# Softmax cross entropy over 32000 classes: labels' load behind the table load, last sums in PSUM, last pieces in multiples of 256 bytes, eight semaphores fewer

## Chip, cores, metric

One core of one Trainium2 chip. The metric is the device time of one execution in microseconds, lower is better. All runs were fast, granted clock 1.0.

## The reference

```python
batch, seq, vocab = 16, 512, 32000          # logits float32, labels int32
logits_max = np.max(logits, axis=-1, keepdims=True)
log_sum_exp = np.log(np.sum(np.exp(logits - logits_max), axis=-1)) + logits_max.squeeze(-1)
log_probs = logits - log_sum_exp[..., np.newaxis]
loss = -log_probs[np.arange(batch)[:, None], np.arange(seq), labels]
```

8192 rows of 32000 logits are read once, 1048.6 MB. The kernel leaves out the maximum (the logits are normal draws) and computes log(sum(exp(x))) - x[label].

## The kernel before

Each of the 128 partitions has 64 rows, "groups" here. A group is loaded in two loads of 16000 columns, into three buffers of 64 kB per partition in turn. ScalarE takes the exp in place and adds it up into one column of `sums`, for which an accumulator read (ACTIVATION_READ_ACCUMULATOR in the profiles) follows each exp; GpSimd picks the labels' logits out of the buffer before that. The first group comes in four loads. The last two groups are cut into ever smaller pieces, so that little is left to do when the last byte has landed.

```python
    plan(0, [[4000, 4000, 8000], [16000]], [(0, 0), (0, 1), (0, 2), (1, 0)])
    for g in range(1, G - 2):
        plan(g, [[W], [W]], [(0, 0), (1, 0)])
    b = loads[-1][1] + 1
    for g, i, at, n in [                    # group, buffer, first column in it, columns
        (G - 2, 0, 0, 12000), (G - 2, 1, 0, 11000), (G - 2, 2, 0, 9000),
        (G - 1, 3, 0, 8720), (G - 1, 2, 9000, 6470), (G - 1, 3, 8720, 4700),
        (G - 1, 4, 0, 3410), (G - 1, 3, 13420, 2550), (G - 1, 4, 3410, 1910), (G - 1, 4, 5320, 1455),
        (G - 1, 4, 6775, 1135), (G - 1, 4, 7910, 905), (G - 1, 4, 8815, 745),
    ]:
        loads.append((g, b + i, at, n))
    # ... cut ...
    sums = persist.tile([P, G - 1, 5], FP32)
    sums_last = persist.tile([P, K], FP32)              # K = 10 pieces of the last group
    # ... cut ...
    nc.scalar.dma_start(out=labs64[:], in_=labels_pg)
    nc.scalar.preload_act_table_set("natural_log_exp_and_others")
    # ... cut: indices, lists and masks for picking the labels' logits ...
    def exp(g, ap):
        k = n_exp.get(g, 0)
        n_exp[g] = k + 1
        s = sums[:, g, k:k + 1] if g < G - 1 else sums_last[:, k:k + 1]
        return nc.scalar.activation(out=ap, in_=ap, func=EXP, accum_out=s)

    for j, (g, b, at, n) in enumerate(loads):
        # ... cut ...
        load = nc.sync.dma_start(out=t[:, at:at + n], in_=lg_pg[:, g, c0:c0 + n])
        if n == W:                                      # three semaphores for full loads,
            n_full[b % 3] += 1                          # one more for each short load
            loaded = (full_in[b % 3], 16 * n_full[b % 3])
        else:
            loaded = (tc.alloc_semaphore(f"short{j}_in"), 16)
        # ... cut: pick on GpSimd, exp on ScalarE, waits ...
        left = len(loads) - 1 - j
        if left == 9:
            nc.vector.reduce_sum(out=totals[:], in_=sums[:], axis=X)
            # ... cut ...
        if left == 8:
            nc.scalar.activation(out=logsum[:], in_=totals[:], func=LN)
            # ... cut ...
        if left == 1:
            nc.vector.reduce_sum(out=part[:], in_=sums_last[:, 0:K - 1], axis=X)
    nc.sync.dma_start(out=out_pg[:, 0:G - 1], in_=res[:])

    nc.scalar.activation(out=logsum_last[:], in_=sums_last[:, K - 1:K], func=LN, bias=part[:])
    nc.vector.tensor_tensor(out=res_last[:], in0=logsum_last[:], in1=lab_logit[:, G - 1:G], op=ALU.subtract)
    nc.sync.dma_start(out=out_pg[:, G - 1:G], in_=res_last[:])
```

The softmax here doesn't subtract the row's maximum and nothing guards it: scores larger than these inputs give would overflow.

Of the kernel before, what the change touches and what calls it, by code (L numbers as in the profile page):

```python
# [9 lines left out]
FP32 = mybir.dt.float32  # L10
# [4 lines left out]
LN = mybir.ActivationFunctionType.Ln  # L15
ALU = mybir.AluOpType
X = mybir.AxisListType.X
# [3 lines left out]
def kernel(  # L21
# [6 lines left out]
    nc = tc.nc  # L28

    B, S, V = logits.shape  # L30
    P = 128
    G = B * S // P
    W = 16000
# [9 lines left out]
    loads = []  # L43

    def plan(g, widths_by_buffer, order):

        n_buffers = 1 + max((l[1] for l in loads), default=-1)
        for b, i in order:
            ws = widths_by_buffer[b]
            loads.append((g, n_buffers + b, sum(ws[:i]), ws[i]))  # L50

    plan(0, [[4000, 4000, 8000], [16000]], [(0, 0), (0, 1), (0, 2), (1, 0)])
    for g in range(1, G - 2):
        plan(g, [[W], [W]], [(0, 0), (1, 0)])
    b = loads[-1][1] + 1
    for g, i, at, n in [
        (G - 2, 0, 0, 12000), (G - 2, 1, 0, 11000), (G - 2, 2, 0, 9000),
        (G - 1, 3, 0, 8720), (G - 1, 2, 9000, 6470), (G - 1, 3, 8720, 4700),
        (G - 1, 4, 0, 3410), (G - 1, 3, 13420, 2550), (G - 1, 4, 3410, 1910), (G - 1, 4, 5320, 1455),
        (G - 1, 4, 6775, 1135), (G - 1, 4, 7910, 905), (G - 1, 4, 8815, 745),  # L60
    ]:
        loads.append((g, b + i, at, n))
    assert sum(l[3] for l in loads) == G * V


    ends = ctx.enter_context(tc.tile_pool(name="ends", bufs=1))
# [2 lines left out]
    persist = ctx.enter_context(tc.tile_pool(name="persist", bufs=1))  # L69
# [26 lines left out]
    in_first = persist.tile([P, G], mybir.dt.int32)  # L96
    picks = ctx.enter_context(tc.tile_pool(name="picks", bufs=2))
    K = 10
    sums = persist.tile([P, G - 1, 5], FP32)
    sums_last = persist.tile([P, K], FP32)  # L100
    totals = persist.tile([P, G - 1], FP32)
    logsum = persist.tile([P, G - 1], FP32)
    res = persist.tile([P, G - 1], FP32)
    part = persist.tile([P, 1], FP32)
    logsum_last = persist.tile([P, 1], FP32)
    res_last = persist.tile([P, 1], FP32)

    ctx.enter_context(tc.manual_schedule())


    nc.scalar.dma_start(out=labs64[:], in_=labels_pg)
    nc.scalar.preload_act_table_set("natural_log_exp_and_others")  # L112
    nc.vector.memset(sums[:], 0.0)  # L113
    nc.gpsimd.iota(idx[:], pattern=[[V, G]], base=0, channel_multiplier=G * V)
    nc.gpsimd.tensor_tensor(out=idx[:], in0=idx[:], in1=labs32, op=ALU.add)  # L115
    nc.gpsimd.iota(part16[:], pattern=[[0, 1]], base=0, channel_multiplier=1)
    nc.gpsimd.iota(entries[:], pattern=[[1, NI]], base=0, channel_multiplier=0, allow_small_or_imprecise_dtypes=True)
    for g in gathered:
        nc.gpsimd.indirect_dma_start(  # L119
            out=lab_logit[:, g:g + 1],  # L120
            out_offset=None,
            in_=lg,
# [6 lines left out]
    for q in range(3):  # L129
        nc.vector.tensor_scalar(  # L130
            out=mine[:, q:q + 1], in0=part16f[:], scalar1=4.0 * q, scalar2=None, op0=ALU.add
        )
    for n in (12.0, 6.0):
        nc.vector.tensor_scalar(  # L134
            out=mine_at[:], in0=mine[:], scalar1=n, scalar2=n, op0=ALU.is_ge, op1=ALU.mult
# [3 lines left out]
    for q in range(3):  # L139
        nc.vector.tensor_scalar(  # L140
            out=mine_at[:, q:q + 1], in0=mine[:, q:q + 1], scalar1=16.0 * q, scalar2=None, op0=ALU.mult
# [4 lines left out]
        out=one_hot[:], in0=entries[:], scalar1=at_entry[:], scalar2=None, op0=ALU.is_equal  # L146
    )
    nc.vector.tensor_scalar(
        out=clamped[:, 0, :], in0=labs32, scalar1=float(W - 1), scalar2=None, op0=ALU.min
    )  # L150
    nc.vector.tensor_scalar(
        out=clamped[:, 1, :], in0=labs32, scalar1=float(-W), scalar2=0.0, op0=ALU.add, op1=ALU.max
    )
    nc.vector.tensor_scalar(
        out=in_first[:], in0=labs32, scalar1=float(W), scalar2=None, op0=ALU.is_lt
    )
    for h in range(2):
        for q in range(3):
            nc.vector.tensor_scalar(  # L159
                out=lists[:, :, h, q], in0=clamped[:, h, :], scalar1=mine[:, q:q + 1], scalar2=None, op0=ALU.mult  # L160
# [6 lines left out]
    buffers = {}  # L167
    col = {}
    n_exp = {}
    full_in = [tc.alloc_semaphore(f"full{i}_in") for i in range(3)]  # L170
    n_full = [0, 0, 0]
    spaces = [data.tile([P, W], FP32, tag=f"t{i}", name=f"t{i}") for i in range(3)]
    exps = []

    def exp(g, ap):
        k = n_exp.get(g, 0)
        n_exp[g] = k + 1
        s = sums[:, g, k:k + 1] if g < G - 1 else sums_last[:, k:k + 1]
        return nc.scalar.activation(out=ap, in_=ap, func=EXP, accum_out=s)  # L179

    for j, (g, b, at, n) in enumerate(loads):
        if b not in buffers:
            buffers[b] = spaces[b % 3]
        t = buffers[b]
        c0 = col.get(g, 0)
        col[g] = c0 + n
        load = nc.sync.dma_start(out=t[:, at:at + n], in_=lg_pg[:, g, c0:c0 + n])  # L187
        if n == W:
            n_full[b % 3] += 1
            loaded = (full_in[b % 3], 16 * n_full[b % 3])  # L190
        else:
            loaded = (tc.alloc_semaphore(f"short{j}_in"), 16)
        load.then_inc(loaded[0], 16)
        tc.no_tile_sem_insts.add(load.ins.name)
        users = []
        if g in picked:
            h = c0 // W
            i = picked.index(g) % NB
            if h == 0 and i == 0:
                pk = picks.tile([P, NB * 2, NI], FP32, tag="pk", name="pk")  # L200
            pick = nc.gpsimd.indirect_copy(  # L201
                out=pk[:, 2 * i + h, :], data=t[:], idxs=lists[:, g, h, 0:3], i_know_this_is_slow=True
            )
            users.append(pick)
        users.append(exp(g, t[:, at:at + n]))
        users[0]._wait_ge(*loaded)
        tc.add_to_no_dep_group(f"load{j}", load.ins)
        tc.declare_no_dep(users[0].ins, load.ins, reason="waits for the load's own semaphore")
        tc.declare_fence(users[0].ins, group=f"load{j}")
        exps.append(users[-1])  # L210
        if g in picked and h == 1 and i == NB - 1:
            nc.vector.copy_predicated(own[:], one_hot[:].unsqueeze(1).to_broadcast([P, NB * 2, NI]), pk[:])  # L212
            nc.vector.reduce_sum(  # L213
                out=found[:, :, g - NB + 1:g + 1].rearrange("p h g -> p g h"),
                in_=own[:].rearrange("p (g h) n -> p g h n", h=2),
                axis=X,
# [5 lines that stand above are left out]
            lo, hi = picked[0], picked[-1] + 1  # L222
            nc.vector.tensor_copy(out=lab_logit[:, lo:hi], in_=found[:, 1, lo:hi])
            nc.vector.copy_predicated(lab_logit[:, lo:hi], in_first[:, lo:hi], found[:, 0, lo:hi])  # L224
        if left == 8:
            nc.scalar.activation(out=logsum[:], in_=totals[:], func=LN)  # L226
            nc.vector.tensor_tensor(out=res[:], in0=logsum[:], in1=lab_logit[:, 0:G - 1], op=ALU.subtract)  # L227
        if left == 1:
            nc.vector.reduce_sum(out=part[:], in_=sums_last[:, 0:K - 1], axis=X)  # L229
    assert n_exp[G - 1] == K  # L230
    nc.sync.dma_start(out=out_pg[:, 0:G - 1], in_=res[:])

    nc.scalar.activation(out=logsum_last[:], in_=sums_last[:, K - 1:K], func=LN, bias=part[:])  # L233
    nc.vector.tensor_tensor(out=res_last[:], in0=logsum_last[:], in1=lab_logit[:, G - 1:G], op=ALU.subtract)  # L234
    nc.sync.dma_start(out=out_pg[:, G - 1:G], in_=res_last[:])

# [29 lines left out]
```

## Time and profile before

| | kernel before |
|---|---|
| time, median of the first 3 runs | 2426.2 us (2426.05 to 2426.23) |
| span of the profiled execution | 2424.19 us |
| that execution's time less its span | 2.20 us |
| mean distance of the landings of full loads (8.19 MB) | 18.87 us |
| last full load landed, last load landed | 2344.10, 2420.18 us |

The span goes from the program's first recorded instruction to its last; the time of a run also holds what the runtime does around it. Landings are the moments at which a load's semaphore, the counter that its transfer raises, is full; they come from the trace's semaphore records, and an exp that waited for data starts 0.02 us after one.

From the page of the kernel before: the span, the chain that ended last by engine, and the issue-to-landing time of the full loads.

```profile
span 2424.2 us, 667 instructions
...
DMA 71%; ACT 23%; issue 4%; POOL 1%; SPq 0%; POOLq 0%; DVE 0%
...
t<-in_logits_dram SPq DMA_DIRECT2D x123, 8000.0 KB, 41.5
```

The chain's 71% for DMA is a lower bound: while it walks over an exp, the transfers go on. 41.5 us from issue to landing is 2.2 times the 18.87 us that a load takes, so two others stand ahead of it in the queue, one of them nearly done.

The start, in order of time (start, duration, engine and line, operation, output and input; in brackets the idle time before it and what ended it):

```profile
0.73 0.40 ACTq L111 DMA_DIRECT2D labs<-in_labels_dram  x1
...
1.16 1.28 ACT L112 ACT_TABLE_LOAD   x1 [1.16 <-PEq L250]
...
8.51 0.32 POOL L115 TENSOR_TENSOR idx<-idx,labs 128x64 int32<-128x64 int32 x1 [7.48 <-DMA labs<-in_labels_dram]
```

The labels' load is issued first, the table load after it, and the labels are there at 8.5 us. The last full load's exp, from the same view, later:

```profile
2344.13 13.54 ACT L179 ACTIVATE t<-t 128x16000 f32<-128x16000 f32 x1 [5.26 <-DMA t<-in_logits_dram]
```

It started as its load landed.

### The profile page before, as it was taken

The page shows a single profiled execution, that of the slowest core. Times are in us where ns is not written, and L with a number is a line of the kernel's source. Part 1 is how long each engine was busy: PE and PEld are TensorE (multiplying, and loading weights), DVE is VectorE, ACT ScalarE, POOL GpSimd, SP SyncE. Part 2 cuts the span into 40 slices and gives each one's busy share as a digit, 9 for nine tenths or more (in the row PEclk, how much of TensorE's full clock was granted, in tenths as well). Part 3 has the DMA queues.
Part 4 walks back from the last instruction along what each step waited for, and adds up shares of the span by engine and source line. Part 5 has one row for each costly group of instructions (what it writes and reads, how often), then busy time and mean ns, then how long its engine had stood idle before and what let it go on. Part 6 is the DMA issues. An engine that isn't in the chain of part 4 may idle for free.

```text
span 2424.2 us, 667 instructions
## 1 busy us (share of the span) xinstructions
DVE 20.5 (1%) x45; ACT 1748.6 (72%) x281; POOL 86.6 (4%) x132
## 2 busy tenths in 40 slices
DVE  0000000000000000000000000000000000000000
ACT  4777767777677767777677776777767776777778
POOL 0000000000000000000000000000000000000000
DMA  9999999999999999999999999999999999999999
GB/s 424 438 423 439 439 423 438 439 430 432 439 437 425 439 438 423 439 438 429 434 439 436 426 439 436 426 439 437 429 435 438 434 429 438 437 426 439 437 430 384
DMA packets 20580, 1048.72 MB, mean 433 GB/s; under 512 B 2656, under 2 KB 2784, under 8 KB 3424
## 3 DMA queue, kind: packets, MB, share of 16 engines
q1 hardware_dynamic: 20304, 1048.62, 99.9%
q10 hardware_dynamic: 144, 0.07, 0.0%
q0 software_dynamic: 128, 0.00, 0.0%
q14 instruction: 4, 0.03, 0.0%
HBM read 1048.64 MB, written 0.03 MB: 433 GB/s over the span
## 4 chain that ended last, share of the span: by engine, by line
DMA 71%; ACT 23%; issue 4%; POOL 1%; SPq 0%; POOLq 0%; DVE 0%
DMA t<-in_logits_dram 71%; ACT t L179 23%; POOL pk L201 1%; SPq L187 0%; POOLq L261 0%; ACT logsum_last L233 0%; ACT logsum L226 0%; DVE res_last L234 0%; POOLq L201 0%
## 5 line engine op out<-in xcount | busy, mean ns | idle before, releaser
L179 ACT ACTIVATE t<-t 128x16000 f32<-128x16000 f32 (+6 forms) x139 | 1734.7, 12480 | 671.8 <-POOL pk L201 630.9
L201 POOL INDIRECT_COPY pk<-t,lists 128x48 f32 x120 | 81.6, 680 | 2211.8 <-DMA t<-in_logits_dram 2211.8
L212 DVE COPY_PREDICATED own<-one_hot,pk 128x960 f32<-128x960 int32 x6 | 7.4, 1235 | 2281.7 <-POOL pk L201 2281.7
L179 ACT ACTIVATION_READ_ACCUMULATOR t<-t 128x1 f32 x139 | 25.9, 186 | 0.0
L213 DVE TENSOR_REDUCE found<-own 128x20 f32<-128x960 f32 x6 | 6.9, 1155 | 0.2
L119 POOL DMA_INDIRECT lab_logit<-in_logits_dram,idx x4 | 4.1, 1032 | 1.3 <-issue 0.9
L112 ACT ACT_TABLE_LOAD x1 | 1.3, 1283 | 1.2 <-PEq L250 1.2
L159 DVE TENSOR_SCALAR lists<-clamped,mine 128x64 uint16<-128x64 f32 x6 | 1.2, 362 | 0.0
L221 DVE TENSOR_REDUCE totals<-sums 128x63 f32<-128x315 f32 x1 | 0.5, 481 | 79.4 <-ACT t L179 79.4
L162 DVE MEMSET own<- 128x960 f32 x1 | 0.9, 858 | 0.1
L115 POOL TENSOR_TENSOR idx<-idx,labs 128x64 int32<-128x64 int32 x1 | 0.3, 319 | 7.5 <-DMA labs<-in_labels_dram 7.5
L145 DVE TENSOR_SCALAR one_hot<-entries,at_entry 128x48 int32<-128x48 f32 x1 | 0.4, 355 | 0.1
L227 DVE TENSOR_TENSOR res<-logsum,lab_logit 128x63 f32<-128x63 f32 x1 | 0.2, 225 | 15.2 <-ACT logsum L226 15.2
L134 DVE TENSOR_SCALAR mine_at<-mine 128x3 f32<-128x3 f32 x2 | 0.3, 169 | 0.1
L113 DVE MEMSET sums<- 128x315 f32 x1 | 0.3, 321 | 0.9 <-PEq L250 0.9
L137 DVE TENSOR_TENSOR mine<-mine,mine_at 128x3 f32<-128x3 f32 x2 | 0.3, 163 | 0.1
L233 ACT ACTIVATE logsum_last<-sums_last,part 128x1 f32<-128x1 f32 x1 | 0.3, 294 | 0.0
L229 DVE TENSOR_REDUCE part<-sums_last 128x1 f32<-128x9 f32 x1 | 0.2, 163 | 14.5 <-ACT t L179 14.5
L140 DVE TENSOR_SCALAR mine_at<-mine 128x1 f32<-128x1 f32 x3 | 0.3, 148 | 0.0
L130 DVE TENSOR_SCALAR mine<-part16f 128x1 f32<-128x1 f32 x3 | 0.3, 147 | 0.0
L226 ACT ACTIVATE logsum<-totals 128x63 f32<-128x63 f32 x1 | 0.2, 238 | 0.0
L224 DVE COPY_PREDICATED lab_logit<-in_first,found 128x60 f32<-128x60 int32 x1 | 0.2, 231 | 0.0
(17 smaller groups left out, 2.7 us busy)
## 6 DMA issues: line engine op xcount, KB each, us to landing
t<-in_logits_dram SPq DMA_DIRECT2D x123, 8000.0 KB, 41.5
t<-in_logits_dram SPq DMA_DIRECT2D x1, 6000.0 KB, 36.8
t<-in_logits_dram SPq DMA_DIRECT2D x1, 5500.0 KB, 32.3
t<-in_logits_dram SPq DMA_DIRECT2D x1, 4500.0 KB, 24.1
t<-in_logits_dram SPq DMA_DIRECT2D x1, 4360.0 KB, 23.6
t<-in_logits_dram SPq DMA_DIRECT2D x2, 2000.0 KB, 9.6
t<-in_logits_dram SPq DMA_DIRECT2D x1, 4000.0 KB, 21.2
t<-in_logits_dram SPq DMA_DIRECT2D x1, 3235.0 KB, 30.9
```

The source lines that it names most:

```text
L112: nc.scalar.preload_act_table_set("natural_log_exp_and_others")
L113: nc.vector.memset(sums[:], 0.0)
L115: nc.gpsimd.tensor_tensor(out=idx[:], in0=idx[:], in1=labs32, op=ALU.add)
L119: nc.gpsimd.indirect_dma_start(out=lab_logit[:, g:g + 1], out_offset=None, in_=lg, in_offset=bass.IndirectOffsetOnAxis(ap=idx[:, g:g + 1], ...
L145: nc.vector.tensor_scalar(out=one_hot[:], in0=entries[:], scalar1=at_entry[:], scalar2=None, op0=ALU.is_equal)
L159: nc.vector.tensor_scalar(out=lists[:, :, h, q], in0=clamped[:, h, :], scalar1=mine[:, q:q + 1], scalar2=None, op0=ALU.mult)
L162: nc.vector.memset(own[:], 0.0)
L179: return nc.scalar.activation(out=ap, in_=ap, func=EXP, accum_out=s)
L201: pick = nc.gpsimd.indirect_copy(out=pk[:, 2 * i + h, :], data=t[:], idxs=lists[:, g, h, 0:3], i_know_this_is_slow=True)
L212: nc.vector.copy_predicated(own[:], one_hot[:].unsqueeze(1).to_broadcast([P, NB * 2, NI]), pk[:])
L213: nc.vector.reduce_sum(out=found[:, :, g - NB + 1:g + 1].rearrange("p h g -> p g h"), in_=own[:].rearrange("p (g h) n -> p g h n", h=2), a ...
L221: nc.vector.reduce_sum(out=totals[:], in_=sums[:], axis=X)
```

## The change

Its intent: start the logits' load before the labels', save the overhead of two loads, make every piece begin and end on 256 bytes, make ScalarE's accumulator reads at the end cheaper by writing them to PSUM in place of SBUF, the core's other on-chip memory (in banks of their own, so that VectorE can sum one part while ScalarE writes another), fit the pieces to the cheaper reads, and leave the closing clear fewer semaphores.

```diff
-    plan(0, [[4000, 4000, 8000], [16000]], [(0, 0), (0, 1), (0, 2), (1, 0)])
-    for g in range(1, G - 2):
+    for g in range(G - 2):
         plan(g, [[W], [W]], [(0, 0), (1, 0)])
@@
-        (G - 2, 0, 0, 12000), (G - 2, 1, 0, 11000), (G - 2, 2, 0, 9000),
-        (G - 1, 3, 0, 8720), (G - 1, 2, 9000, 6470), (G - 1, 3, 8720, 4700),
-        (G - 1, 4, 0, 3410), (G - 1, 3, 13420, 2550), (G - 1, 4, 3410, 1910), (G - 1, 4, 5320, 1455),
-        (G - 1, 4, 6775, 1135), (G - 1, 4, 7910, 905), (G - 1, 4, 8815, 745),
+        (G - 2, 0, 0, 11264), (G - 2, 1, 0, 10752), (G - 2, 2, 0, 9984),
+        (G - 1, 3, 0, 9152), (G - 1, 3, 9152, 6656), (G - 1, 2, 9984, 4736),
+        (G - 1, 4, 0, 3392), (G - 1, 4, 3392, 2496), (G - 1, 4, 5888, 1728), (G - 1, 4, 7616, 1408),
+        (G - 1, 4, 9024, 1024), (G - 1, 4, 10048, 768), (G - 1, 4, 10816, 640),
@@
-    sums = persist.tile([P, G - 1, 5], FP32)
-    sums_last = persist.tile([P, K], FP32)
+    psum = ctx.enter_context(tc.tile_pool(name="psum", bufs=1, space=bass.MemoryType.PSUM))
+    sums = persist.tile([P, G - 1, 3], FP32)
+    sums_last = psum.tile([P, 8, 512], FP32, tag="sums_last", name="sums_last")
+    place_last = [(max(0, k - 2), min(k, 2) if k <= 2 else 0) for k in range(K)]
@@
+    nc.scalar.preload_act_table_set("natural_log_exp_and_others")
     nc.scalar.dma_start(out=labs64[:], in_=labels_pg)
-    nc.scalar.preload_act_table_set("natural_log_exp_and_others")
     nc.vector.memset(sums[:], 0.0)
+    nc.vector.memset(sums_last[:, :, 0:K - 7], 0.0)
@@
-        s = sums[:, g, k:k + 1] if g < G - 1 else sums_last[:, k:k + 1]
+        if g < G - 1:
+            s = sums[:, g, k:k + 1]
+        else:
+            bank, at = place_last[k]
+            s = sums_last[:, bank, at:at + 1]
@@
-        if n == W:
-            n_full[b % 3] += 1
-            loaded = (full_in[b % 3], 16 * n_full[b % 3])
+        if at == 0:
+            count_in[b % 3] += 16
+            loaded = (first_in[b % 3], count_in[b % 3])
         else:
-            loaded = (tc.alloc_semaphore(f"short{j}_in"), 16)
+            loaded = (tc.alloc_semaphore(f"load{j}_in"), 16)
@@
-            nc.vector.reduce_sum(out=part[:], in_=sums_last[:, 0:K - 1], axis=X)
+            nc.vector.reduce_sum(out=partial[:], in_=sums_last[:, 0:7, 0:K - 7], axis=mybir.AxisListType.XY)
@@
-    nc.scalar.activation(out=logsum_last[:], in_=sums_last[:, K - 1:K], func=LN, bias=part[:])
+    nc.scalar.activation(out=logsum_last[:], in_=sums_last[:, 7, 0:1], func=LN, bias=partial[:])
```

(Names of tiles and an assertion are cut.) The pieces 0, 1 and 2 of the last group share bank 0; pieces 3 to 9 have banks 1 to 7.

More of the change, by code (lines that the diff above doesn't have):

```diff
@@ L56 @@
     for g, i, at, n in [
-        (G - 2, 0, 0, 12000), (G - 2, 1, 0, 11000), (G - 2, 2, 0, 9000),
-        (G - 1, 3, 0, 8720), (G - 1, 2, 9000, 6470), (G - 1, 3, 8720, 4700),
-        (G - 1, 4, 0, 3410), (G - 1, 3, 13420, 2550), (G - 1, 4, 3410, 1910), (G - 1, 4, 5320, 1455),
-        (G - 1, 4, 6775, 1135), (G - 1, 4, 7910, 905), (G - 1, 4, 8815, 745),
+        (G - 2, 0, 0, 11264), (G - 2, 1, 0, 10752), (G - 2, 2, 0, 9984),
+        (G - 1, 3, 0, 9152), (G - 1, 3, 9152, 6656), (G - 1, 2, 9984, 4736),
+        (G - 1, 4, 0, 3392), (G - 1, 4, 3392, 2496), (G - 1, 4, 5888, 1728), (G - 1, 4, 7616, 1408),
+        (G - 1, 4, 9024, 1024), (G - 1, 4, 10048, 768), (G - 1, 4, 10816, 640),
     ]:
         loads.append((g, b + i, at, n))
-    assert sum(l[3] for l in loads) == G * V
+    assert sum(l[3] for l in loads) == G * V and all(l[2] % 64 == l[3] % 64 == 0 for l in loads)
     ends = ctx.enter_context(tc.tile_pool(name="ends", bufs=1))
@@ L103 @@
     res = persist.tile([P, G - 1], FP32)
-    part = persist.tile([P, 1], FP32)
+    partial = persist.tile([P, 1], FP32)
     logsum_last = persist.tile([P, 1], FP32)
@@ L169 @@
     n_exp = {}
-    full_in = [tc.alloc_semaphore(f"full{i}_in") for i in range(3)]
-    n_full = [0, 0, 0]
+    first_in = [tc.alloc_semaphore(f"first{i}_in") for i in range(3)]
+    count_in = [0, 0, 0]
     spaces = [data.tile([P, W], FP32, tag=f"t{i}", name=f"t{i}") for i in range(3)]
-    exps = []
     def exp(g, ap):
@@ L209 @@
         tc.declare_fence(users[0].ins, group=f"load{j}")
-        exps.append(users[-1])
         if g in picked and h == 1 and i == NB - 1:
```

## The prediction

> **What bounds the kernel now.** I read the page first (busy shares, transfer rate), then the waits, then the order of time at both ends, then the packet records under it.
>
> From the page:
>
> ```profile
> DVE 20.5 (1%) x45; ACT 1748.6 (72%) x281; POOL 86.6 (4%) x132
> ...
> DMA  9999999999999999999999999999999999999999
> GB/s 424 438 423 439 439 423 438 439 430 432 439 437 425 439 438 423 439 438 429 434 439 436 426 439 436 426 439 437 429 435 438 434 429 438 437 426 439 437 430 384
> ...
> q1 hardware_dynamic: 20304, 1048.62, 99.9%
> ```
>
> No engine is near full, and the transfers are busy in every slice. The logits are 8192 x 32000 x 4 B = 1048.6 MB, read once; only the last slice, with 384 GB/s, is below the rest. So the time is: first byte, 1048.6 MB at the rate of the transfers, then what is left after the last byte. The queue of the loads, from the waits of SyncE:
>
> ```profile
> SPq L187 <- ACT t L179: 2333.3, 126, 26.4
> ```
>
> The loads are issued when the exp of a buffer ends, but they take 41.5 us to land while 8.2 MB take 18.87 us (mean distance of landings in the trace), so two loads always stand in the queue and this wait costs nothing. The chain of waits gives 71% to the transfers and 23% to the exps because it walks from an exp to the load that it released; it must not be read as 23% of exps to be saved.
>
> The tail, in order of time:
>
> ```profile
> 2392.22 7.47 ACT L179 ACTIVATE t<-t 128x8720 f32<-128x8720 f32 x1 [2.54 <-DMA t<-in_logits_dram]
> 2399.60 0.19 ACT L179 ACTIVATION_READ_ACCUMULATOR t<-t 128x1 f32 x1
> 2399.90 5.59 ACT L179 ACTIVATE t<-t 128x6470 f32<-128x6470 f32 x1
> 2405.40 0.19 ACT L179 ACTIVATION_READ_ACCUMULATOR t<-t 128x1 f32 x1
> 2405.50 0.24 ACT L226 ACTIVATE logsum<-totals 128x63 f32<-128x63 f32 x1
> 2405.64 4.10 ACT L179 ACTIVATE t<-t 128x4700 f32<-128x4700 f32 x1
> ...
> 2420.23 0.18 ACT L179 ACTIVATION_READ_ACCUMULATOR t<-t 128x1 f32 x1
> 2420.32 0.81 ACT L179 ACTIVATE t<-t 128x745 f32<-128x745 f32 x1
> 2420.45 0.16 DVE L229 TENSOR_REDUCE part<-sums_last 128x1 f32<-128x9 f32 x1 [14.46 <-ACT t L179]
> 2421.04 0.18 ACT L179 ACTIVATION_READ_ACCUMULATOR t<-t 128x1 f32 x1
> 2421.26 0.29 ACT L233 ACTIVATE logsum_last<-sums_last,part 128x1 f32<-128x1 f32 x1
> 2421.58 0.16 DVE L234 TENSOR_TENSOR res_last<-logsum_last,lab_logit 128x1 f32<-128x1 f32 x1 [0.97 <-ACT logsum_last L233]
> 2421.77 0.34 SPq L235 DMA_DIRECT2D out_dram<-res_last  x1
> ```
>
> The reader is to see that ScalarE waits for data before the 8720 piece and has no gap from the 6470 piece on. By the landing records the 6470 piece landed at 2399.88 and the 745 piece at 2420.18, so each of the last eight exps starts 0.10 to 0.20 us after its data: the tail is balanced between transfers and ScalarE, with ScalarE 0.14 us late at the end. Everything that is left to save is: under 1 us there, some tenths of transfer time, some tenths at the two ends.
>
> **What the Trainium skill says.** (1) "Perfetto Trace Analysis", Optimizing Scalar/DVE Operations: a ScalarE operation carries about 93 ns of data access on SBUF and about 51 on PSUM, and the latency in a profile is about twice that. The trace agrees for SBUF: an accumulator read is 186 ns long, and the next exp starts 93 ns after it. That PSUM is shorter no run has shown yet. (2) "DMA: Bandwidth & Descriptors", How a descriptor splits into AXI transactions: pieces go in units of 256 B, and a start off such a boundary fetches unused bytes. The packet records agree in kind: 64000 B take 2361 ns and 16000 B 596, so a packet costs 7.7 ns + 0.03677 ns/B; the off-boundary 2980 B should then take 117 and take 122, 3620 B 141 and take 142, 13640 B 509 and take 511. (3) The same page, Queues, rings and completion order: an engine alternates between its queues packet by packet. Below. (4) "PSUM — Partial Sum Buffer", PSUM bank collisions raise a hardware error: two engines must not touch one bank at once. So the VectorE sum of the first pieces and the last accumulator go to different banks; no cost follows.
>
> **The change part by part.** A load is 128 rows on 16 DMA engines, 8 packets each.
>
> - *First group in two loads in place of four.* Before, buffer 0 took per engine 8 x (596 + 596 + 1185) = 19.02 us, now 8 x 2361 = 18.89. On the path: -0.13 us. The first exp moves from 8.2 us to about 21 us (1.75 for the first packet + 0.5 of slow first packets + 18.9); ScalarE has 5.2 us idle per load and its buffer is needed again at about 58 us, so nothing follows.
> - *Labels behind the table load.* They are 512 B packets, nine per engine with the completion, 27 ns each: 0.24 us of transfer time in either place. They now alternate with 2.36 us packets in place of 0.6 us ones, so they should land near 9 x 2.4 + 2.5 = 24 us (8.2 before). First use at 61 us: hidden. The first logits packet came 1.0 us after its issue with the labels issued beside it; the last store, alone, also took 0.95. At most -0.06 us; I take -0.02.
> - *Multiples of 256 B.* Excess over the line 7.7 + 0.03677 B times 8, summed over the last pieces: 38 (745), 8 (905), 3, 3, 10 and less, about 0.1 us in all. The landing of the last piece: -0.1 us.
> - *Accumulators in PSUM.* An exp with its read occupies ScalarE for N/1.2 ns + 186 (4700: 4.10; 1910: 1.78). If PSUM shortens the read's share from 93 to 51, that is N/1.2 + 144. The new sizes say that this was assumed: the old ones follow "exp of a piece = transfer of the next" at 186 ns within 30 columns, the new ones do so at about 130 to 145.
> - *The new sizes.* I ran the tail by hand: a piece starts at its landing + 0.02 or when ScalarE is free; 0.14 for the logarithm of the other groups after the second piece. Old sizes, 186: the last exp with its read is done 0.93 us after the last landing (the trace: 0.95, at 2421.13). New sizes: at 144, 0.95; at 186, 1.33; at 131, 0.83. The first three accumulators share a bank, and the order of instructions shows that the second and third exp now wait for the one before to be complete; the second waits for its data anyway, the third may lose about 0.05. So I expect 0.98: +0.03.
> - *The last logarithm.* The accumulator read before it should be 144 long in place of 186, and the logarithm (294) reads PSUM: -0.08. VectorE's sum over seven banks is longer than 163 ns but has 0.6 us.
> - *Eight semaphores fewer.* The kernel's closing clear of its semaphores takes 222 ns for about 33; 8 of them: -0.05 us if it is proportional.
>
> Sum: -0.13 - 0.02 - 0.10 + 0.03 - 0.08 - 0.05 = -0.35. From 2426.2: **2425.85 us**.
>
> **The rivals.** *PSUM shortens only the write's end, not ScalarE's period.* For it: the accumulator read has no source operand in the trace, and the 93 ns may belong to the reading side. Then the new sizes are wrong for the machine, the tail grows by 0.38 in place of 0.03 and the time is about 2426.2. I give it three in ten. *The tail gets shorter than I think:* period 100 ns or less over N/1.2; by the same hand run the end is then 0.65 after the last landing, and the time 2425.5. Against it: nothing in the skill goes so low. *The labels or the four gathers disturb the large packets*, since they now lie beside 64 kB packets: their bytes are the same, so I give this little; it would cost some tenths. *The new order starves the queue at the end:* the load of 3392 columns waits for the exp of 10752, done near 2379, when more than 25 us of transfers are still queued; so no.
>
> **Range and chances.** The three runs of before lie within 0.2 us. The sum of my uncertain terms is about 0.5 us either way, and another chip may add some: 2425.0 to 2426.7. A change of 2% is 48 us; nothing here reaches it unless the bandwidth changes, so within 2% 0.99, faster 0.005, slower 0.005.
>
> **What would show it.** In the profile of after: 20016 packets on the logits' queue (139 transfers x 144) with the same distance of 18.87 us between landings; labels landing near 24 us; accumulator reads of the last group near 144 ns, with the next exp about 51 ns after the read's start (93 would mean the first rival); the last exp starting 0.2 to 0.35 us after its landing; last logarithm near 250 ns; semaphore clear under 200 ns. I am wrong if the loads' rate differs, if ScalarE's lateness grows from piece to piece past 0.4 us, or if a wait for the piece before costs more than 0.1 us.

## The result

The changed kernel took 2425.90 us (median of 6 runs, 2425.80 to 2425.97); the kernel before 2426.23 in the same rounds (6 runs, 2426.05 to 2426.60). The ratio, computed as the mean time of one kernel's fast runs over that of the other's of the same rounds and so not quite the ratio of these medians, is 0.9998, with an interval of 0.9985 to 1.0011. The measured 2425.90 lies within 0.05 us of the forecast of 2425.85. Whether for the forecast's reasons is the rest of this document.

The page after: the span, the transfer rate in 40 slices, and the logits' queue.

```profile
span 2424.1 us, 663 instructions
...
GB/s 424 437 425 439 439 423 438 439 428 434 439 435 427 439 436 426 439 439 427 435 439 433 429 439 435 427 439 438 425 438 438 431 432 438 435 428 439 436 426 389
...
q1 hardware_dynamic: 20016, 1048.62, 99.9%
```

139 transfers of 144 packets: 20016. But the span has shrunk by only 0.12 us (2424.19 to 2424.07 in the trace's own figures), the time of these two executions by 0.49. 2.20 us of the kernel before lay outside the span, 1.83 of the changed one.

The start, in order of time:

```profile
0.73 1.28 ACT L114 ACT_TABLE_LOAD   x1 [0.73 <-PEq L256]
...
0.77 0.39 ACTq L115 DMA_DIRECT2D labs<-in_labels_dram  x1
...
22.84 0.32 POOL L119 TENSOR_TENSOR idx<-idx,labs 128x64 int32<-128x64 int32 x1 [21.82 <-DMA labs<-in_labels_dram]
```

The sequencer does not wait for the table load: the labels' load is issued 0.04 us later than before. GpSimd has the labels at 22.8 us in place of 8.5, because their small packets now take turns with packets of 64 kB. The Trainium skill's "DMA: Bandwidth & Descriptors", Queues, rings and completion order, says that an engine changes between its queues at packet boundaries, and this is that: from 4.66 us on, the labels' queue gets one packet per engine every 2.38 us, eight times, with the completion in the last turn (the prediction counted nine).

The tail, in order of time:

```profile
2343.91 13.54 ACT L186 ACTIVATE t<-t 128x16000 f32<-128x16000 f32 x1 [5.24 <-DMA t<-in_logits_dram]
...
2400.23 0.15 ACT L186 ACTIVATION_READ_ACCUMULATOR t<-t 128x1 f32 x1
2400.47 5.75 ACT L186 ACTIVATE t<-t 128x6656 f32<-128x6656 f32 x1
2406.13 0.15 ACT L186 ACTIVATION_READ_ACCUMULATOR t<-t 128x1 f32 x1
2406.18 0.24 ACT L232 ACTIVATE logsum<-totals 128x63 f32<-128x63 f32 x1
2406.37 4.15 ACT L186 ACTIVATE t<-t 128x4736 f32<-128x4736 f32 x1
...
2420.30 0.20 ACT L186 ACTIVATION_READ_ACCUMULATOR t<-t 128x1 f32 x1
2420.36 0.78 ACT L186 ACTIVATE t<-t 128x640 f32<-128x640 f32 x1
...
2420.98 0.21 ACT L186 ACTIVATION_READ_ACCUMULATOR t<-t 128x1 f32 x1
2421.22 0.26 ACT L239 ACTIVATE logsum_last<-sums_last,partial 128x1 f32<-128x1 f32 x1
...
2421.71 0.34 SPq L241 DMA_DIRECT2D out_dram<-res_last  x1
```

Three things differ from the lines before. The exp of the 6656 piece starts 0.24 us after the accumulator read ahead of it, though ScalarE was free and the data were there at 2400.34. The accumulator reads grow from 0.15 us to 0.21. And the 640 piece, landed at 2419.72, is begun at 2420.36, 0.63 us after its landing ("late" below), where the last piece of the kernel before was 0.14 late. What did come as planned is the period: the 640 exp starts 0.05 us after the start of the read ahead of it, where that took 0.09 before.

Where the difference of the two profiled executions lies, from the landing and instruction records:

| stretch | before | after | difference |
|---|---|---|---|
| start to landing of the last full load | 2344.10 | 2343.89 | -0.21 |
| to the last landing | 76.08 | 75.83 | -0.25 |
| to the end of the last accumulator read | 1.04 | 1.47 | +0.43 |
| to the issue of the last store | 0.55 | 0.52 | -0.03 |
| to the closing clear of the semaphores | 1.90 | 1.88 | -0.02 |
| clear and end of the span | 0.52 | 0.48 | -0.04 |
| outside the span | 2.20 | 1.83 | -0.37 |

### The profile page after: what moved, and what is told of

The parts are those of the page before. It is cut to its first block, busy times and chain, and to the rows that moved or that the text cites. A ratio compares the mean times of both kernels' runs of the same rounds, so it can differ in the third digit from the quotient of the medians.

```text
span 2424.1 us, 663 instructions
## 1 busy us (share of the span) xinstructions
DVE 20.4 (1%) x46; ACT 1747.6 (72%) x277; POOL 87.3 (4%) x132
## 2 busy tenths in 40 slices
DMA packets 20292, 1048.72 MB, mean 433 GB/s; under 512 B 2624, under 2 KB 2752, under 8 KB 3392
## 4 chain that ended last, share of the span: by engine, by line
DMA 71%; ACT 24%; issue 3%; POOL 1%; SPq 0%; DVE 0%; ACTq 0%; POOLq 0%
DMA t<-in_logits_dram 71%; ACT t L186 24%; POOL pk L208 1%; SPq L194 0%; ACT logsum_last L239 0%; DVE res_last L240 0%; ACT logsum L232 0%; ACTq L186 0%; POOLq L208 0%
## 5 line engine op out<-in xcount | busy, mean ns | idle before, releaser
L186 ACT ACTIVATE t<-t 128x16000 f32<-128x16000 f32 (+4 forms) x137 | 1734.1, 12661 | 673.1 <-POOL pk L208 630.4
```

## The experiments

Theory one (the forecast's): the gain is the sum of small steps inside the span: fewer and aligned packets, cheaper reads, fewer semaphores. Theory two (from the table): inside the span the tail has become longer, and the gain is something outside the span that has to do with none of the change's intents. The first row of the table could be chance; the first experiment asks that.

All figures: median of 5 runs of the experiment, 9 runs of the kernel before in the same rounds. "Tail" is from the landing of the last full load to the end of the last accumulator read. "Outside" is time less span, from the profiled execution; the unprofiled runs, whose spans are listed to 0.1 us, agree within 0.06.

| experiment | VectorE instructions | time | before, same rounds | tail, of it to the last landing | outside |
|---|---|---|---|---|---|
| kernel before (first profile) | 63 | | 2426.23 | 77.12, 76.08 | 2.20 |
| changed kernel (first profile) | 64 | 2425.90 | 2426.23 | 77.30, 75.83 | 1.83 |
| after_again | 64 | 2426.08 | 2426.22 | 77.30, 75.83 | 1.83 |
| labels_first | 64 | 2425.89 | 2426.22 | 77.31, 75.83 | 1.83 |
| four_loads | 64 | 2426.02 | 2426.22 | 77.31, 75.85 | 1.83 |
| sbuf_sums | 63 | 2426.56 | 2426.22 | 77.45, 75.85 | 2.20 |
| before_memset | 64 | 2426.24 | 2426.51 | 77.13, 76.09 | 1.83 |
| one_less | 63 | 2426.25 | 2426.51 | 77.32, 75.84 | 2.19 |
| banks_reversed | 64 | 2425.97 | 2426.51 | 77.32, 75.84 | 1.83 |
| old_sizes | 64 | 2425.61 | 2426.51 | 77.01, 76.10 | 1.83 |
| bank_order | 64 | 2425.76 | 2426.33 | 77.13, 75.84 | 1.83 |
| old_aligned | 64 | 2425.46 | 2426.33 | 76.82, 75.84 | 1.83 |
| before_two | 65 | 2425.99 | 2426.33 | 77.12, 76.09 | 1.97 |

The rows from before_memset to old_sizes ran on another chip than the four above them, and the last three on a third. On the second chip the kernel before spread over 0.9 us (2426.14 to 2427.03). So times of different rounds are compared with care.

### after_again: the changed kernel once more

No edit.

> The changed kernel once more, to learn what repeats. All theories: 0.2 to 0.4 us under the kernel before in the same rounds (2425.9 against 2426.2). If the steps that the landings took around an instruction fetch (one of +0.14 us near 406 us and one of +0.68 near 1614 us in the first profile, against +0.50 and +0.68 in the kernel before) belong to the program, they come again at the same loads and of the same size; if they are chance, they differ by some tenths.

2426.08 us (2425.90 to 2426.16). The tail came again to 0.01 us and "outside" to 0.00. The landing of the last full load did not: 2344.14 in place of 2343.89. The steps at the instruction fetches are partly chance. The packet records show four fetches on the instruction queue while the loads run, 8192 B each; in the changed kernel they came at 406, 800, 1420 and 1614 us. The load in flight at the first was late by 0.14 us in the first profile and by 0.6 in this one; the one at 1614 was late by 0.68 both times, the one at 800 by nothing. So some tenths of any single profile before the tail are chance, and the first row of the table (-0.21) says nothing.

### labels_first: the labels' load ahead of the table load again

```diff
-    nc.scalar.preload_act_table_set("natural_log_exp_and_others")
     nc.scalar.dma_start(out=labs64[:], in_=labels_pg)
+    nc.scalar.preload_act_table_set("natural_log_exp_and_others")
```

> The changed kernel with the labels' load issued ahead of the table load again, as before. The prediction's step: +0.02 us at most 0.06, labels still landing near 22 us because they alternate with 64 kB packets. Rival from the two traces (the third landing came 0.18 us later after the change though 0.13 of packet time was saved, so the small packets among large ones cost 0.3): no difference either, unless it is the place behind the table load that did it; then 0.2 to 0.3 us faster than the changed kernel.

2425.89 us against 2426.08 of after_again on the same chip; their ranges overlap (2425.75 to 2426.06). First packet of logits at 1.76 us, 1.75 in the changed kernel; labels landed at 22.8. This part of the change does nothing that these runs can see.

### four_loads: the first group in four loads again

```diff
-    for g in range(G - 2):
+    plan(0, [[4000, 4000, 8000], [16000]], [(0, 0), (0, 1), (0, 2), (1, 0)])
+    for g in range(1, G - 2):
```

(with four columns in `sums` in place of three)

> The changed kernel with the first group's rows in four loads again (4000, 4000, 8000, 16000 columns), labels left behind the table load, two semaphores more. The prediction's step: 0.13 us slower from packet overhead (+0.01 for two semaphores). Rival: the labels and gathers then alternate with 16 kB and 32 kB packets, land near 8 us, and the landing of the third full load comes 0.1 to 0.2 us earlier than in the changed kernel, so the time is 0.1 to 0.2 us shorter.

2426.02 us (2425.84 to 2426.23), after_again 2426.08. The labels land at 8.4 us again, so it is the size of the packets beside them that delays them, not the table load. The fourth 16000 columns had landed at 79.24 us; in the two-load kernels of the same chip they came at 79.12, 79.47 and 79.30 (after_again, labels_first, sbuf_sums), which is neither theory. The saving of 0.13 us is inside the noise. Over all profiles the last full load landed at 2343.84 to 2344.14 in the nine with two loads (mean 2343.95) and at 2343.85 to 2344.58 in the four with four loads (mean 2344.11): the sign fits, the spread is larger than the difference. Left open.

### sbuf_sums: the last sums in SBUF again, new sizes kept

```diff
-    sums_last = psum.tile([P, 8, 512], FP32, tag="sums_last", name="sums_last")
+    sums_last = persist.tile([P, K], FP32)
@@
-    nc.vector.memset(sums_last[:, :, 0:K - 7], 0.0)
@@
-            s = sums_last[:, bank, at:at + 1]
+            s = sums_last[:, k:k + 1]
```

(the reduction and the logarithm read it accordingly)

> The changed kernel with the last group's sums in SBUF again, new sizes kept. If PSUM saves 42 ns of ScalarE's period per piece, ten of them: the hand run of the tail gives 1.33 us from the last landing to the end of the last exp at 186 ns against 0.95 at 144. But the changed kernel also lost about 0.15 us to the second and third piece waiting for the one before (same bank), which SBUF does not have. So 0.2 to 0.3 us slower than the changed kernel; accumulator reads of 186 ns, next exp 93 ns after the read's start; no gap before the second piece's exp beyond its landing. If PSUM brings nothing: same time or faster by 0.1.

2426.56 us, 0.48 slower than after_again, more than expected. From its tail, in order of time:

```profile
2400.21 0.19 ACT L184 ACTIVATION_READ_ACCUMULATOR t<-t 128x1 f32 x1
2400.34 5.75 ACT L184 ACTIVATE t<-t 128x6656 f32<-128x6656 f32 x1
...
2421.12 0.19 ACT L184 ACTIVATION_READ_ACCUMULATOR t<-t 128x1 f32 x1
```

The second exp starts 0.13 us after the read's start and 0.02 after its landing: without the shared bank it does not wait. All reads take 0.19. The tail is 0.14 us longer than in the changed kernel: what PSUM's shorter period saves, less what the wait for the shared bank costs. The other 0.37 lie outside the span: 2.20 again. So either PSUM itself or the one VectorE instruction that went with it (the memset) decides what happens outside the span.

### before_memset: the kernel before with one idle VectorE instruction

```diff
     nc.vector.memset(sums[:], 0.0)
+    nc.vector.memset(part[:], 0.0)
```

> The kernel before with one VectorE memset of a 128x1 tile added near the start, a tile that is written again before it is read: 64 instructions for VectorE in the program in place of 63, nothing else changed. It is there because the time that lies outside the profiled span was 2.20 us in the two kernels with 63 (before, sums in SBUF) and 1.83 in the four with 64, while the span itself hardly moved. If the number of VectorE instructions decides it: 0.3 to 0.4 us faster than the kernel before (2425.85), the span unchanged, time less span 1.83. If it is PSUM or the order of the end that decides it: the time of the kernel before (2426.2), time less span 2.20.

"Outside" is 1.83 us in the profiled execution and 1.80 to 1.84 in all five runs, against 2.15 to 2.24 in the nine of the kernel before. By medians it was 0.27 us faster, 2426.24 against 2426.51. The first line of its page:

```profile
span 2424.7 us, 668 instructions
```

Its time was 2426.50; it happened to be the slowest of the five. Nothing in the change's list is in this kernel; a memset that nobody needs brings, outside the span, the 0.37 us that the change brought there. The times alone would not show it: the two ranges overlap (2425.82 to 2426.50 and 2426.14 to 2427.03).

### one_less: the changed kernel with one VectorE instruction fewer

```diff
-    nc.vector.reduce_sum(out=at_entry[:], in_=mine_at[:], axis=X)
-    nc.vector.tensor_tensor(out=at_entry[:], in0=at_entry[:], in1=part16f[:], op=ALU.add)
+    nc.vector.reduce_sum(out=at_entry[:], in_=mine_at4[:], axis=X)     # part16f is its fourth column
```

> The changed kernel with one VectorE instruction fewer (an add of 128x1 at the start folded into the reduction before it): 63 in place of 64; PSUM sums, sizes, semaphores and loads as changed. By the count: 0.3 to 0.4 us slower than the changed kernel, 2426.3, time less span 2.20, span 2424.1. By PSUM: 2425.95 as the changed kernel, time less span 1.83.

2426.25 us (2426.22 to 2426.36). Its page:

```profile
span 2424.1 us, 662 instructions
```

The span is that of the changed kernel, "outside" is 2.19 (2.14 to 2.22 in the five runs). banks_reversed, which ran beside it and has 64, had 2425.97. With PSUM, sizes, loads and semaphores of the change in place, the gain is gone when VectorE has 63 instructions.

### before_two: the kernel before with two idle VectorE instructions

```diff
     nc.vector.memset(sums[:], 0.0)
+    nc.vector.memset(part[:], 0.0)
+    nc.vector.memset(part[:], 0.0)
```

> The kernel before with two VectorE memsets of 128x1 added: 65 instructions for VectorE. With 63 the time less the span was 2.20 us in every run, with 64 it was 1.83. If 64 is a threshold: 1.83 again. If it is even against odd: 2.20 again. If it is a matter of where the end stands in a larger block, something else may come, within 0.5 us.

"Outside" was 1.97 (1.93 to 2.01), neither of the two values, and the time 2425.99 against 2426.33. So it is neither a threshold at 64 nor even against odd. One record bears on where the 0.37 lie: after the span's end there is one last packet of 8192 B on the instruction queue, and it comes 1.67 to 1.68 us after the end in the three profiles with 63 VectorE instructions, 1.18 to 1.20 in the nine with 64. That is 0.49 sooner, more than the 0.37, and with 65 the fetch came at 1.14, the earliest, though "outside" was 1.97. So something ahead of this fetch differs, but the fetch is not the whole of it. The counts of the other engines in the built programs do not sort the runs: the kernel before and before_memset differ in VectorE's alone. Why the number of VectorE instructions decides it, no record says; it stays open.

### old_sizes: the sizes of before, PSUM kept

```diff
-        (G - 1, 3, 0, 9152), (G - 1, 3, 9152, 6656), (G - 1, 2, 9984, 4736),
+        (G - 1, 3, 0, 8720), (G - 1, 2, 9000, 6470), (G - 1, 3, 8720, 4700),
         # ... and so on down to 745, as before; group G - 2 too
```

> The changed kernel with the piece sizes of before (12000, 11000, 9000 and 8720 down to 745), not multiples of 64 columns; PSUM kept. By the prediction's steps: the last landing 0.1 us later from the lost 256 B multiples, the end of the last exp 0.79 us after it in place of 0.95, so 0.06 faster in all. By the trace of the changed kernel, where the last exp ended 1.41 after its landing because lateness grew from 0.02 to 0.63: the old sizes at 145 ns a piece stay late by under 0.25, so the end is 0.2 to 0.4 us nearer to the last landing; if the last landing is 0.1 to 0.25 later, the time is 0.0 to 0.25 us shorter than the changed kernel.

2425.61 us (2425.51 to 2425.73), 0.36 faster than banks_reversed, the changed kernel's equal in the same rounds. The tail is 77.01 us, 0.29 shorter, though the last landing comes 0.27 later in it. From its tail:

```profile
2416.60 0.15 ACT L186 ACTIVATION_READ_ACCUMULATOR t<-t 128x1 f32 x1
2416.67 1.42 ACT L186 ACTIVATE t<-t 128x1455 f32<-128x1455 f32 x1
...
2420.86 0.15 ACT L186 ACTIVATION_READ_ACCUMULATOR t<-t 128x1 f32 x1
```

ScalarE is back to waiting for data: the read of the 1910 piece starts at 2416.60 and the next exp not 0.05 but 0.07 after it, when its data have landed (by the records; 1910 and the next three pieces start 0.02 after their landing, the last 0.03). Where ScalarE has paused the read takes 0.15 us, also at the very end (2420.86). So most of ScalarE's lateness comes from the new proportions and not from PSUM as such; bank_order below finds 0.17 us of it in the shared bank.

### banks_reversed: the last piece in bank 0

```diff
-    place_last = [(max(0, k - 2), ...
+    place_last = [(7 - max(0, k - 2), ...
```

> The changed kernel with the banks in reverse: the first three pieces in bank 7, the last piece in bank 0. In the changed kernel the accumulator reads took 153 ns for bank 0 and 162, 170, 178, 187, 195, 204, 212 for banks 1 to 7. If the bank's place sets that, the last read takes 153 in place of 212 and the end comes 0.06 us sooner, with the first three reads at 212. If it is the time or the order, the reads grow again towards the end and nothing is gained.

The reads grow towards the end as before, though bank 7 now comes first and bank 0 last:

```profile
2400.28 0.15 ACT L186 ACTIVATION_READ_ACCUMULATOR t<-t 128x1 f32 x1
...
2421.04 0.21 ACT L186 ACTIVATION_READ_ACCUMULATOR t<-t 128x1 f32 x1
```

0.153 for the first three, then 0.160 to 0.206 (0.212 in the changed kernel). So it is not the bank's place. With old_sizes' reads it follows that a read gets some 8 ns longer with each piece that ScalarE takes without a pause, and falls back to 0.153 after a pause. The next exp still starts 0.051 us after the read's start, so a longer read costs nothing until the last one, for which the last logarithm waits: there it costs up to 0.06 us.

### bank_order: no bank shared with the piece just before

```diff
-    place_last = [(max(0, k - 2), min(k, 2) if k <= 2 else 0) for k in range(K)]
+    place_last = [(k, 0) for k in range(7)] + [(0, 1), (1, 1), (7, 0)]
```

> The changed kernel with the sums of the last group's ten pieces in banks 0 to 6, then 0 and 1 again, then 7, in place of three in bank 0 and then 1 to 7: no piece shares a bank with the one just before it, so the wait of the second and third exp for the one before falls away. My theory: the second piece's exp starts 0.02 us after its landing in place of 0.13, the third is late by 0.28 or less in place of 0.39, and as ScalarE has no gap after that the end comes 0.11 to 0.15 us sooner: 2425.83 where the changed kernel has 2425.95. The prediction's step said 0.05. Rival: the wait costs nothing because other waits stand beside it; then nothing changes.

2425.76 us against 2426.33 of the kernel before. From its tail:

```profile
2400.27 0.15 ACT L186 ACTIVATION_READ_ACCUMULATOR t<-t 128x1 f32 x1
2400.40 5.75 ACT L186 ACTIVATE t<-t 128x6656 f32<-128x6656 f32 x1
...
2420.84 0.22 ACT L186 ACTIVATION_READ_ACCUMULATOR t<-t 128x1 f32 x1
```

The second exp starts 0.13 us after the read in place of 0.24, and 0.02 after its landing. The tail is 77.13 us, 0.17 shorter than in the changed kernel. The instructions show the cause: with the first three sums in one bank, the built program has a wait ahead of the second and the third exp, for the semaphore that ScalarE's own reads raise, until the piece before is complete; here it has none there. It is a wait for two writes in a row to one PSUM bank, though they go to different columns. (Pieces 7 and 8 come back to banks 0 and 1 here and are given such a wait too, but for writes that are long done: they start 51 ns after the read ahead of them, like the others.) Against sbuf_sums, which has the same sizes and no such wait either, PSUM alone makes the tail 0.31 us shorter (77.13 against 77.45).

### old_aligned: the sizes of before, rounded to 64 columns

```diff
-        (G - 1, 3, 0, 9152), (G - 1, 3, 9152, 6656), (G - 1, 2, 9984, 4736),
+        (G - 1, 3, 0, 8704), (G - 1, 2, 9024, 6464), (G - 1, 3, 8704, 4672),
         # ... 3392, 2560, 1920, 1472, 1152, 896, 768; group G - 2: 11968, 11008, 9024
```

> The changed kernel with the sizes of before rounded to multiples of 64 columns (11968, 11008, 9024, 8704, 6464, 4672, 3392, 2560, 1920, 1472, 1152, 896, 768), so alignment without the new proportions. From the landing of the last full load to the last landing it was 76.1 us with the old sizes (three kernels) and 75.83 with the new ones (four kernels). The prediction's alignment term: 0.1 us of it, so 76.0, and 0.1 faster than the run with old sizes (2425.5 after 2425.6). Rival one: alignment is all of it, 75.85 and 0.25 faster. Rival two: it is the smaller last pieces, 76.1 and no gain.

2425.46 us (2425.30 to 2425.83) against 2426.33: the fastest kernel here, 0.87 under the kernel before and 0.30 under bank_order by medians of the same rounds. To the last landing it took 75.84 us: rival one. Alignment alone is worth 0.26 us there, as much with 768 columns at the end as with 640.

```profile
2419.95 0.88 ACT L186 ACTIVATE t<-t 128x768 f32<-128x768 f32 x1
...
2420.69 0.21 ACT L186 ACTIVATION_READ_ACCUMULATOR t<-t 128x1 f32 x1
```

The last piece is 0.04 late. The tail of 76.82 us is the shortest measured.

The packet records split the 0.25. The last piece's last packet ended 75.62 to 75.64 us after the landing of the last full load in the four profiles with the old sizes, 75.53 to 75.55 in the nine with multiples of 256 B: 0.09, the prediction's 0.1. From there to the landing it took 0.45 to 0.46 us against 0.29 to 0.32: another 0.16, which no step named. What fills this time no record says.

### Not measured

Two further versions joined bank_order's banks and the logarithm of the other groups moved ahead of the last group's first exp, where ScalarE is idle for 2.2 us in the changed kernel. One (refitted) had newly cut sizes, 9024, 6464, 4672 and so on down to 704; the other (joined) had those of old_aligned. No chip ran them, so nothing is said of their times; old_aligned is the best version that was measured. Eight semaphores were not tried by themselves: the closing clear took 222 ns in every profile of a kernel with the semaphores of before and 178 in every other one but four_loads (two semaphores more, 182). So eight fewer go with 44 ns and two more with 4, not one price for each.

## Why the prediction was right, step by step

The number was right, 2425.85 for 2425.90. Its reasons were not, in the main: the steps inside the span, as they really went, come to about +0.1 us for everything from the last full load on, and the gain that is sure came from outside the span, which no step named.

| step of the prediction | said | measured | by |
|---|---|---|---|
| first group in two loads | -0.13 | not to be told from chance | four_loads, thirteen profiles |
| labels behind the table load | -0.02 | nothing seen; labels at 22.7 us (about 24 said) | labels_first |
| multiples of 256 B, last landing | -0.10 | -0.25 | 76.08 to 76.10 in four profiles, 75.83 to 75.85 in nine |
| new sizes and PSUM, from the last landing until ScalarE could begin a next exp | +0.03 | +0.36 | tail of the two traces |
| last read and last logarithm | -0.08 | +0.04 (read +0.07, logarithm -0.03) | tail of the two traces |
| eight semaphores fewer | -0.05 | -0.04 | length of the clear |
| number of VectorE instructions | not named | -0.37 | before_memset, one_less, sbuf_sums |

- *Two loads, labels.* Harmless, as said, and too small to be seen. (The first load landed at 22.5 us, where its exp was said to begin at about 21.)
- *Alignment.* The mechanism was right, the size was off: 0.25 us at the landing where 0.10 was said. The step read the excess from the duration of packets, and the packets do end 0.09 earlier; the other 0.16 lie between the last packet and the landing (old_aligned).
- *New sizes and PSUM.* This is the step that failed, in its sum and not in its period. The period was right: the next exp starts 93 ns after a read in SBUF and 51 after one in PSUM, which are the figures of the Trainium skill ("Perfetto Trace Analysis", Optimizing Scalar/DVE Operations). From the 3392 piece on, a piece of N columns in the changed kernel holds ScalarE for N/1.2 ns + 143 to 144, and 144 was said. So the first rival, that PSUM would not shorten the period, is refuted. But by the hand run ScalarE would be free 0.98 us after the last landing, and it was free after 1.31. The 0.33 add up when the hand run is done again beside the trace. First, 0.17 are the landings: from that of the 6656 piece to the last it took 19.38 us, 19.55 by the packet line. Then 0.14 are the shared bank: its wait cost 0.17 and not 0.03 (bank_order). The last 0.02 are the logarithm of the other groups, 0.16 in place of 0.14. As to the landings, each packet took what the line says (102 ns for 2560 B), but landings follow one another faster than the durations add up. The full loads show this too: eight packets of 2361 ns make 18.89 us, and they land 18.86 apart (median), some 3.6 ns less for each packet. Why is not shown. And since ScalarE, apart from the bank's waits, has no gap from the 6656 piece on, landings that came earlier than said brought nothing: what the alignment row has more than forecast comes back in this one.
- *The last read and the logarithm.* The logarithm went from 294 to 261 ns, nearly as said. The read before it became longer, not shorter: 185 to 212 ns, where 144 was said. That 144 is what a piece's period has above N/1.2 ns, not the length of a read; twice the page's 51 would be 102. The last read now ends 0.16 us after the moment at which a next exp could begin, 0.09 before.
- *Semaphores.* 44 ns for eight, as said; that the clear goes by their number is not shown.
- *Its own signs of being wrong.* The prediction named two that came: lateness past 0.4 us (0.63), and a wait for the piece before of more than 0.1 us (0.17).
- *What was missing.* The forecast took the 2 us outside the span for constant. It is constant for one program, to 0.1 us, but not from program to program. Without the instruction that came with PSUM the change would have had only what the span gives, and there it is 0.1 us behind from the last full load on. one_less is that kernel; its time, 2426.25, can't be set against the kernel before to a tenth, because that one spread over 0.9 us in the same rounds (median 2426.51).

The number came out by luck, because two errors were of nearly one size: the steps from the last full load to the end of the span were said to bring -0.20 and brought +0.09, and the -0.37 outside was not said at all. The -0.15 of the start can't be told from chance.

## What to carry to other kernels

When a change is worth tenths of a microsecond, cut the profile at fixed events and compare the stretches; the sum can be right while each part is wrong, and the part that paid can be one that nobody meant. Compare time less span between the kernels as well, and try one idle instruction on the quietest engine before crediting a change with 0.3 us. A tail in which transfers and an engine keep step must be fitted to landings that were measured, not to packet durations added up. And look for waits in the built program: two accumulators in a row in one PSUM bank were given one here, even in different columns.

## What the Trainium skill lacked or had wrong

- "Perfetto Trace Analysis", Optimizing Scalar/DVE Operations: the 93 and 51 ns agree with the start of the next exp after an accumulator read. That the latency in a profile is about twice this holds for SBUF (186 ns), not for PSUM: 153 ns after a pause, and some 8 ns more with each piece that follows without one, up to 218 (bank_order). No bank's place plays a part (banks_reversed).
- "PSUM — Partial Sum Buffer" speaks of two engines in one bank. It does not tell that two writes in a row of one engine to different columns of a bank may be given a wait on each other in the built program: 0.17 us for two such waits (bank_order).
- "DMA: Bandwidth & Descriptors", How a descriptor splits into AXI transactions, tells the mechanism of alignment but no time: ten pieces of 3 to 35 kB per partition, and three larger ones, landed 0.25 us sooner when all began and ended on 256 B, of which 0.09 had passed when the last packet ended.
- "Runtime: NRT & Kernel Launch", The ~15µs preamble/postamble breakdown: no word that the part outside the program depends on the number of an engine's instructions. Time less span was 2.20 us with 63 instructions for VectorE, 1.83 with 64, 1.97 with 65.
- The same page, Instruction fetch mechanics, calls the cost of a block's fetch mostly hidden. Here it may not be: the load in flight at the last fetch (1577 or 1614 us) landed 0.42 to 0.69 us late in all thirteen profiles, at the others between nothing and 0.6 and not alike from run to run. That the fetch is the cause is argued from its time, which lies 37 us earlier in the programs with two loads more, and the late landing with it; no run moved it alone.
- No page has a time for the program's own closing clear of its semaphores: 222 ns before, 178 with eight fewer, 182 with six fewer.
